# Layer 1's modulation as sums on VectorE, with moved residuals and another square

## The chip, the cores and the metric

The kernel runs on one core of one Trainium2 chip. The metric is the device time of one execution in microseconds. An execution computes two transformer blocks for 256 tokens of x (S = 256) and 256 tokens of context, model width D = 1024, all in 32-bit floats.

## The reference

Only what the change touches is kept. The first block is one layer of dilated window attention with its own modulation. The second has two layers: layer 0 mixes by retention and a gated scan, layer 1 by window attention, and each is followed by an MLP. In layer 1 the context only supplies keys and values, so its gates and its second shift and scale are not needed.

```python
def modulation(cvec, w, b):
    m = jax.nn.silu(cvec) @ w + b
    return jnp.split(m[..., None, :], 6, axis=-1)
def sublayer_residual(x, y, gate, g, b):
    return layer_norm(DEEPNORM_ALPHA * x + gate * y, g, b)
def sq_relu_mlp(h, w1, w2):
    return jnp.square(jax.nn.relu(h @ w1)) @ w2

for i in range(DEPTH_2):
    sh1, sc1, g1, sh2, sc2, g2 = modulation(c, w_mod[i], b_mod[i])
    csh1, csc1, cg1, csh2, csc2, cg2 = modulation(c_ctx, w_mod[i], b_mod[i])
    h = x * (1.0 + sc1) + sh1
    hc = xc * (1.0 + csc1) + csh1
    ...
    x = sublayer_residual(x, y, g1, ln_g[i, 0], ln_b[i, 0])
    x = sublayer_residual(x, sq_relu_mlp(x * (1.0 + sc2) + sh2, mlp_w1[i], mlp_w2[i]), g2, ln_g[i, 1], ln_b[i, 1])
    ...
```

## The kernel before, in words

**Stages.** The first block takes the first 330 us or so; the mixer of layer 0 follows; layer 0's MLP (512 tokens: context and x) runs from about 640 to 1053 us, layer 1's attention to 1195, layer 1's MLP (256 tokens) to the end at 1416.

**Order.** Each engine has one queue, worked off in order. A scheduler with a timeline simulation of its own sets the order when the kernel is built; tile pools with numbered buffers and, where given, `issue_after` edges bound what it may do. The order is fixed before the run.

**Weights and GEMMs.** Every weight of a GEMM comes in pieces of 128x1024 (`wload`): SyncE's queue loads `raw` (4 buffers), ScalarE rounds it into `whi` (L133), VectorE subtracts to get `wlo` (L134). `w_a` and `w_b` load the pieces of one weight. Each product is three matmuls (`mm3`, L157 to L159). In layer 0's MLP one `w_a` or `w_b` serves 48 matmuls of 512 columns. The accumulators are PSUM banks: three of tag `mm`, two of `S`, two of `T` (transposes), one of `O`.

**Fillers.** The modulation is a row vector times a matrix of 1024 columns for each of its parts. `quad` is a generator that streams the matrix (`mvraw`, three buffers of 128x1024, also on SyncE's queue) and multiplies it on TensorE (L239) into bank `O`, in four column tiles of 32 each; the result `R` gets its bias (`mvb`, loaded by POOL's queue), and `to_cols` (L271 and its transposes) makes columns of it. `fill(rate)` at the start of every `w_a` and `w_b` advances the generator by `rate` loads. `finish` runs a begun generator to its end, which the first block does ahead of its attention (both use bank `O`). Layer 0's modulation (`quad` with keys 0, b, c) is filled in during the first block, layer 1's during layer 0's MLP.

**The first block's attention.** For each of four head pairs (called heads below): POOL loads two tables `B` from `tabd` (two buffers), TensorE makes scores `S` (L522), VectorE reduces them with the table (L525, into `pr`, two buffers), ScalarE takes the exponential (L531), TensorE transposes `pr` (L193) and multiplies with the values into bank `O` (L545).

**The MLP.** `mlp` runs eight groups `g` of 512 hidden columns. For a group: `w_a` twice (first weight, 256 columns each), relu on ScalarE (L1001), the square as a multiplication on VectorE (L1002), `split` of the result into `fx` (a rounded half on ScalarE, the rest on VectorE, L110 and L111); then `w_b` twice (second weight), with results copied (`g` = 0, L1013) or added to `y` (L1015) by VectorE. `late` runs after group 0's square: it gives the residual stream its new values (`new_resid`: L954 times the norm's gain row, L955 plus its bias row, 128x1024 each). At the end of layer 0's MLP `after0` makes the next inputs (`modulate`: transposes, ScalarE's `hf`, VectorE's casts `hCh`, `hCh0b` at L303, rest `hCl` at L304) and two new residuals.

Of the kernel before, what the change touches and what calls it, by code (L numbers as in the profile page):

```python
# [95 lines left out]
def body(tc, a, cst, out):  # L96
    nc = tc.nc
    with ExitStack() as ctx:
# [10 lines left out]
        def split(hi, lo, src):  # L109
            nc.scalar.copy(hi, src)  # L110
            nc.vector.tensor_sub(lo, src, hi.bitcast(F32))  # L111
# [14 lines left out]
        rate = [0]  # L126

        def wload(src, k, n):
            raw = wpool.tile([P, 1024], F32, tag="raw", name="raw", bufs=4)
            nc.sync.dma_start(raw.rearrange("p (k n) -> p k n", k=k), src)  # L130
# [3 lines left out]
            nc.vector.tensor_sub(lo, raw, hi.bitcast(F32))  # L134
            return hi.rearrange("p (k n) -> p k n", k=k), lo.rearrange("p (k n) -> p k n", k=k)

        def w_a(w, col, nk=KC):

            fill(rate[0])
            ts = []  # L140
            for k0 in range(0, nk, 4):
                hi, lo = wload(w[k0 * P:(k0 + 4) * P, col:col + 256].rearrange("(k p) n -> p k n", p=P), 4, 256)
                ts += [(hi[:, k], lo[:, k]) for k in range(4)]
            return ts

        def w_b(w, col, nk=KC):

            fill(rate[0])
            ts = []
            for k0 in range(0, nk, 2):  # L150
                hi, lo = wload(w[k0 * P:(k0 + 2) * P, col:col + 512].rearrange("(k p) n -> p k n", p=P), 2, 512)
                ts += [(hi[:, k], lo[:, k]) for k in range(2)]
            return ts
# [56 lines left out]
        nc.gpsimd.memset(neghalf, -0.5)  # L210
        nc.vector.tensor_copy(cst_a[:, :, 0], cv[:, 2, :])
# [12 lines left out]
        def quad(pool, rpool, key, w, col, b, stat, vecs, n=512, rows=""):  # L224
# [32 lines left out]
            if rows:  # L257
# [3 lines left out]
                RD[rows] = rd  # L261
            yield
# [182 lines left out]
        def quad0():  # L445
            yield from quad(p1t, None, "0", w_mod[0], 0, b_mod[0], cst_m, 2)
            m0["a"] = to_cols(R["0"], "m0a")

        fillers.append(quad0())
        fillers.append(quad(p1t, const, "b", w_mod[0], 2048, b_mod[0], cst_m, 2, rows="b0"))  # L450
        fillers.append(quad(p1t, const, "c", w_mod[0], 4096, b_mod[0], cst_m, 2, rows="c0"))
# [132 lines left out]
        m0a = m0["a"]  # L584
        m0b = to_cols(R["b"], "m0b")
        m0c = to_cols(R["c"], "m0c")
# [376 lines left out]
        def mlp(layer, Ts, xks, y, pool, mid, late, norm, after):  # L963
# [4 lines left out]
            for g in range(8):  # L968
                fx = (main, pool)[g % 2].tile([P, 8, n], F32R, tag=("qkb", "fx")[g % 2], name="fx")
                fh, fl = fx[:, 0:4], fx[:, 4:8]  # L970
                if layer and g < 1:
                    ws = w_b(w1, 512 * g)
                    for i in range(2):
# [3 lines left out]
                        nc.vector.tensor_mul(f, f, o)  # L977
# [13 lines left out]
                for i in range(0 if layer and g < 1 else 2):  # L991
                    if g:
                        ws = w_a(w1, 512 * g + 256 * i)
                    for j in range(2):
# [7 lines left out]
                        nc.vector.tensor_mul(f, f, o)  # L1002
# [44 lines left out]
        m1a, m1b = {}, {}  # L1047
        fillers.append(quad(pm, pm, "0", w_mod[1], 0, b_mod[1], cst_m, 2))
        fillers.append(quad(pm, const, "b", w_mod[1], 2048, b_mod[1], cst_m, 2, rows="b1"))
        fillers.append(quad(pm, const, "c", w_mod[1], 4096, b_mod[1], cst_m, 2, rows="c1"))  # L1050
# [14 lines left out]
        rate[0] = 2  # L1065
        mod1 = {}

        def after0(T):
# [194 lines left out]
```

## Time and profile before

| what | us |
|---|---|
| median of 3 runs (1414.46 to 1416.97) | 1416.27 |
| the profiled execution | 1418.32 |
| its span (first to last instruction) | 1416.5 |
| TensorE busy | 1336.0 |
| VectorE busy | 784.4 |
| ScalarE busy | 539.1 |
| mean granted TensorE clock, as a share of full | 0.97 |

Matmuls are pipelined: the duration of one reaches into the next, so busy time of TensorE is not the same as its work. What a matmul adds to a dense row is read from start to start. The share of busy time over the whole span says little here, since the stages differ; tables of stretches come first, single instructions after.

### The profile page before, as it was taken

Reading aid. Unit: us, or ns where it says so; the run is one execution under the profiler, and the core shown is the slowest. Engines: PE = TensorE matmul, PEld = TensorE weight load, DVE = VectorE, ACT = ScalarE, POOL = GpSimd, SP = SyncE. Lnnn points to the kernel's source line nnn. Section 1 sums busy time; section 2 is a strip of 40 time slices with the busy share of each in tenths; the row PEclk is TensorE's granted clock in tenths of the full one; section 3 lists DMA queues with packets and bytes.
Section 4 is the critical chain, followed back from the end, with each engine's and each line's share of the span. In section 5 each row is a group of like instructions: output and inputs, shape, how many; then the busy total and the mean of one; then the engine's idle time right before and its main releaser. Section 6 shows DMA issues by size and latency. Waiting matters only on the chain.

```text
span 1416.5 us, 19846 instructions
## 1 busy us (share of the span) xinstructions
PE 1336.0 (94%) x7918; PEld 1054.8 (74%) x7918; DVE 784.4 (55%) x1312; ACT 539.1 (38%) x859; POOL 89.2 (6%) x138
## 2 busy tenths in 40 slices
PE   6999998999899999898999999999988899799995
PEld 5788865589787777676677767767768777698985
DVE  3534444345824348567444434344677877666666
ACT  2433434335531354214232132223235576454541
POOL 2110021000200200101000000000010000000000
PEclk9999999999989999899999999999998999899998
DMA  9888885565512411327643554553223603365651
GB/s 331 308 276 294 271 276 150 165 210 176 153 60 75 124 46 60 119 74 268 178 134 119 155 178 132 175 174 109 89 96 87 169 16 127 111 206 168 192 178 46
DMA packets 137987, 222.27 MB, mean 157 GB/s; under 512 B 8604, under 2 KB 86012, under 8 KB 137894
## 3 DMA queue, kind: packets, MB, share of 16 engines
q1 hardware_dynamic: 131984, 206.07, 46.1%
q0 software_dynamic: 5168, 14.38, 3.4%
q8 instruction: 62, 1.02, 0.3%
q10 hardware_dynamic: 742, 0.55, 0.1%
q14 instruction: 31, 0.25, 0.1%
HBM read 217.19 MB, written 1.16 MB: 154 GB/s over the span
## 4 chain that ended last, share of the span: by engine, by line
PE 87%; DVE 6%; DMA 3%; issue 2%; ACT 1%; POOL 0%; SPq 0%; DVEq 0%; ACTq 0%; POOLq 0%
PE mm L157 23%; PE mm L158 22%; PE mm L159 22%; PE O L239 5%; PE T L193 2%; DMA mvraw<-in_w_mod_dram 2%; PE mm L415 1%; PE O L1190 1%; PE S L1165 1%; DVE wlo L134 1%; PE S L522 1%; DMA raw<-in_w_in_dram 1%; PE T L747 1%; DVE st L318 1%; PE O L545 1%
## 5 line engine op out<-in xcount | busy, mean ns | idle before, releaser
L134 DVE TENSOR_TENSOR wlo<-raw,whi 128x1024 fp32r<-128x1024 f32 x261 | 318.5, 1223 | 238.1 <-ACT whi L133 236.8
L133 ACT CAST whi<-raw 128x1024 fp32r<-128x1024 f32 x261 | 273.1, 1050 | 444.1 <-PE mm L159 252.7
L157 PE MATMUL mm<-whi,fx 128*128 128x512 f32 x384 | 155.1, 404 | 3.2 <-DVE y L1015 2.2
L158 PE MATMUL mm<-wlo,fx 128*128 128x512 f32 x384 | 151.4, 394 | 0.0
L159 PE MATMUL mm<-whi,fx 128*128 128x512 f32 x384 | 144.8, 396 | 0.1
L157 PEld LDWEIGHTS mm<-whi,fx 128*128 128x128 f32 x384 | 72.2, 188 | 40.0 <-DVE y L1015 12.8
L157 PE MATMUL mm<-A1a,whi 128*128 128x256 f32 x352 | 101.0, 287 | 0.0
L159 PE MATMUL mm<-A1a,wlo 128*128 128x256 f32 x352 | 100.0, 284 | 0.0
L158 PE MATMUL mm<-A1a,whi 128*128 128x256 f32 x352 | 99.9, 284 | 0.0
L158 PE MATMUL mm<-hBl,whi 128*128 128x512 f32 (+1 forms) x256 | 97.3, 381 | 0.0
L239 PE MATMUL O<-mvraw,cst_m 128*32 128x512 f32 x384 | 80.6, 608 | 7.8 <-DMA mvraw<-in_w_mod_dram 7.8
L159 PEld LDWEIGHTS mm<-whi,fx 128*128 128x128 f32 x384 | 72.0, 188 | 19.7 <-issue 2.5
L1015 DVE TENSOR_TENSOR y<-y,mm 128x512 f32<-128x512 f32 x72 | 47.5, 684 | 67.7 <-PE mm L159 67.1
L158 PEld LDWEIGHTS mm<-wlo,fx 128*128 128x128 f32 x384 | 72.3, 188 | 15.1
L157 PEld LDWEIGHTS mm<-A1a,whi 128*128 128x128 f32 x352 | 66.3, 188 | 12.9 <-issue 11.1
L158 PEld LDWEIGHTS mm<-A1a,whi 128*128 128x128 f32 x352 | 66.3, 188 | 6.1 <-issue 6.0
L159 PEld LDWEIGHTS mm<-A1a,wlo 128*128 128x128 f32 x352 | 66.3, 188 | 3.1 <-issue 2.8
L158 PE MATMUL mm<-hDl,whi 128*128 128x256 f32 x224 | 63.0, 281 | 0.0
L1002 DVE TENSOR_TENSOR f<-f,mm 128x512 f32<-128x512 f32 (+1 forms) x58 | 32.2, 555 | 52.8 <-ACT f L1001 52.7
L1001 ACT ACTIVATE f<-mm 128x512 f32<-128x512 f32 (+1 forms) x58 | 28.5, 492 | 79.1 <-PE mm L159 78.0
L158 PEld LDWEIGHTS mm<-hBl,whi 128*128 128x128 f32 x256 | 48.1, 188 | 10.7 <-issue 0.8
L157 PE MATMUL mm<-whi,hA 128*128 128x512 f32 x128 | 51.3, 401 | 0.0
(479 smaller groups left out, 2806.9 us busy)
## 6 DMA issues: line engine op xcount, KB each, us to landing
raw<-in_mlp_w_dram SPq DMA_DIRECT2D x128, 512.0 KB, 4.2
mvraw<-in_w_mod_dram SPq DMA_DIRECT2D x96, 512.0 KB, 4.6
raw<-in_w_in_dram SPq DMA_DIRECT2D x64, 512.0 KB, 6.5
raw<-in_ev_w_in_dram SPq DMA_DIRECT2D x25, 512.0 KB, 4.6
raw<-in_od_w_qkv_dram SPq DMA_DIRECT2D x12, 512.0 KB, 3.5
mvraw<-in_w_ada_dram SPq DMA_DIRECT2D x10, 512.0 KB, 6.9
raw<-in_w_out_dram SPq DMA_DIRECT2D x8, 512.0 KB, 3.9
raw<-in_ev_w_out_dram SPq DMA_DIRECT2D x8, 512.0 KB, 3.8
```

The source lines that it names most:

```text
L133: nc.scalar.copy(hi, raw)
L134: nc.vector.tensor_sub(lo, raw, hi.bitcast(F32))
L157: nc.tensor.matmul(o, lh, rh, start=first, stop=False)
L158: nc.tensor.matmul(o, lh, rl, start=False, stop=False)
L159: nc.tensor.matmul(o, ll, rh, start=False, stop=last)
L193: nc.tensor.transpose(o, i, ident[:n, :n])
L239: nc.tensor.matmul(acc[32 * j:32 * j + 32, :n], stat[:, k, :], raw[:, j * n % 1024:j * n % 1024 + n], start=k == 0, stop=k == KC - 1)
L318: nc.vector.bn_stats(st[:, half, :], r[:, 512 * half:512 * half + 512])
L415: nc.tensor.matmul(o[:, j, :], w_[:, k, js], h_[:, 2 * p + k, :], start=(p, j, k, n) == (0, 0, 0, 0), stop=(p, k, n) == (3, 1, 2), skip_gr ...
L1001: nc.scalar.activation(f, o, AF.Relu)
L1002: nc.vector.tensor_mul(f, f, o)
L1015: nc.vector.tensor_add(y[:, T, hs], y[:, T, hs], o)
```

## The change

Five edits.

1. `fill` moves from ahead of the weights of each `w_a` and `w_b` to behind them (`fill_behind`), with an edge behind the last load of the weight (on SyncE) and behind the last `wlo` (on VectorE).
2. Layer 1's modulation is no longer made by `quad`. A new generator `summed` handles one of six parts at a time (`sh1`, `sc1` for two vectors each, `ga1`, `sh2`, `sc2`, `ga2` for one). It loads the same 48 pieces `mvraw`; VectorE multiplies each by a scalar per partition and adds it to `mva` (8 first products as tensor_scalar, 56 as scalar_tensor_tensor, 128x1024). At the end of a part the partitions are summed by matmuls with `sel` (a column of ones) into bank `O`, four to a vector, 32 in all; VectorE adds the bias, and four of the parts are transposed to columns from there. 96 matmuls of L239 and 12 transposes go. The rate is 0 in group 0's first weight, 2 after its `late`, 3 from group 3 on.
3. The square of relu is an activation on ScalarE.
4. `late` in both MLPs is queued behind `split`. The two new residuals at the end of layer 0's MLP move into layer 1's attention (behind the heads of kv = 2); at the MLP's end ScalarE copies y into their place instead. Their rows of gain and bias take buffers of the attention's pool.
5. In the first block the columns of `quad` b and c are made inside the generator, so `finish` makes those of b.

```diff
+        def fill_behind():
+            if rate[0] and queued:
+                with tc.issue_after(queued["load"]), tc.issue_after(queued["lo"]):
+                    fill(rate[0])
...
         def w_a(w, col, nk=KC):
-            fill(rate[0])
             ts = []
             for k0 in range(0, nk, 4):
                 hi, lo = wload(w[k0 * P:(k0 + 4) * P, col:col + 256].rearrange("(k p) n -> p k n", p=P), 4, 256)
                 ts += [(hi[:, k], lo[:, k]) for k in range(4)]
+            fill_behind()
             return ts
...
+        def summed(pool, res, key, w, col, b, stat, vecs, rows=False):
+            n = D // 4
+            r = pool.tile([P, n], F32, tag="mvb", name="mvb", bufs=1)
+            nc.gpsimd.memset(r, 0.0)
+            for m in range(vecs):
+                nc.gpsimd.dma_start(r[m::32, :], b[col:col + D].rearrange("(j n) -> j n", n=n))
+            accs = [pool.tile([P, D], F32, tag="mva", name="mva", bufs=2) for _ in range(vecs)]
+            wv = w.rearrange("(p k) n -> p k n", k=KC)
+            for k in range(KC):
+                raw = pool.tile([P, D], F32, tag="mvraw", name="mvraw", bufs=3)
+                nc.sync.dma_start(raw, wv[:, k, col:col + D])
+                yield
+                for m, acc in enumerate(accs):
+                    if k:
+                        nc.vector.scalar_tensor_tensor(acc, raw, stat[:, k, m:m + 1], acc, op0=ALU.mult, op1=ALU.add)
+                    else:
+                        nc.vector.tensor_scalar_mul(acc, raw, stat[:, k, m:m + 1])
+            o = bank("O")
+            for m, acc in enumerate(accs):
+                for j in range(4):
+                    nc.tensor.matmul(o[32 * j:32 * j + 32, :n], sel[:, m, :], acc[:, n * j:n * j + n], start=m == 0, stop=m == vecs - 1)
+            nc.vector.tensor_add(r, o[:, :n], r)
...
+                res[key] = to_cols(r, key, "O")
...
-        fillers.append(quad(p1t, const, "b", w_mod[0], 2048, b_mod[0], cst_m, 2, rows="b0"))
-        fillers.append(quad(p1t, const, "c", w_mod[0], 4096, b_mod[0], cst_m, 2, rows="c0"))
+        def quadcols(key, col, rows=""):
+            yield from quad(p1t, None, key, w_mod[0], col, b_mod[0], cst_m, 2, rows=rows)
+            m0[key] = to_cols(R[key], "m0" + key)
+        fillers.append(quadcols("0", 0))
+        fillers.append(quadcols("b", 2048, "b0"))
+        fillers.append(quadcols("c", 4096, "c0"))
...
+                if g == 3:
+                    rate[0] = 3
...
-                        nc.vector.tensor_mul(f, f, o)
+                        nc.scalar.activation(f, f, AF.Square)
...
                 if g == 0:
-                    late()
+                    with tc.issue_after(queued["split"]):
+                        late()
+                    rate[0] = 2
...
             modulate(y0[:, T, :], (mod1["cc"], mod1["cx"])[T // 2], mod1["h"], P * T)
-            if T == 0:
-                for t in (2, 3):
-                    new_resid(t, y0[:, t, :], mod1["ln"])
+            if T > 1:
+                nc.scalar.copy(resid(T), y0[:, T, :])
...
+            if kv == 2:
+                with tc.issue_after(queued["split"]):
+                    for T in (2, 3):
+                        new_resid(T, resid(T), lnr)
```

TensorE where layer 0's MLP begins: the last matmul of the mixer's output projection, the transposes of r, and the first matmuls of group 0. Before:

```order
L159 MATMUL mm<-whi,yL 128x512
L193 MATMUL T<-ident,r_5254 128x128 x8
L239 MATMUL O<-mvraw,cst_m 32x512 x2
L193 MATMUL T<-ident,r_5254 128x128 x4
L239 MATMUL O<-mvraw,cst_m 32x512 x2
L193 MATMUL T<-ident,r_5254 128x128 x4
L157 MATMUL mm<-hBh_5265,whi 128x256 x2
```

The same place after the change:

```order
L167 MATMUL mm<-whi,yL 128x512
L201 MATMUL T<-ident,r_5258 128x128 x16
L165 MATMUL mm<-hBh_5269,whi 128x256 x2
L165 MATMUL S<-hBh_5269,whi 128x256 x2
L166 MATMUL mm<-hBl,whi 128x256
```

The products of the modulation have gone from between the transposes.

VectorE in layer 0's MLP, while y is added up (`y_5652` and `y_5656` are the same tile). Before:

```order
L111 TENSOR_TENSOR fx<-f,fx 128x512
L1015 TENSOR_TENSOR y_5652<-y_5652,mm 128x512 x3
L255 TENSOR_TENSOR R_6415<-O,mvb 128x512
L134 TENSOR_TENSOR wlo<-raw,whi 128x1024
L1015 TENSOR_TENSOR y_5652<-y_5652,mm 128x512
L134 TENSOR_TENSOR wlo<-raw,whi 128x1024
L1015 TENSOR_TENSOR y_5652<-y_5652,mm 128x512 x3
```

After:

```order
L1062 TENSOR_TENSOR y_5656<-y_5656,mm 128x512 x3
L142 TENSOR_TENSOR wlo<-raw,whi 128x1024
L292 SCALAR_TENSOR_TENSOR mva<-mvraw,cst_m,mva 128x1024 x2
L1062 TENSOR_TENSOR y_5656<-y_5656,mm 128x512
L142 TENSOR_TENSOR wlo<-raw,whi 128x1024
L292 SCALAR_TENSOR_TENSOR mva<-mvraw,cst_m,mva 128x1024
L1062 TENSOR_TENSOR y_5656<-y_5656,mm 128x512
L292 SCALAR_TENSOR_TENSOR mva<-mvraw,cst_m,mva 128x1024
L1062 TENSOR_TENSOR y_5656<-y_5656,mm 128x512 x2
```

The multiply-adds of the sums stand among the weights' subtractions and ahead of additions to y.

TensorE in the first block where the attention's products with the values end; the stretch from the last product of `quad` b to that place is longer than can be shown. Before:

```order
L545 MATMUL O<-PT,A0a 64x128 x2
L565 MATMUL T<-qkba 128x256
L239 MATMUL O<-mvraw,cst_m 32x512 x6
L565 MATMUL T<-qkba 128x256 x2
L193 MATMUL T<-ident,Rb 128x128 x4
```

After, where `quad` b's products end:

```order
L167 MATMUL mm<-A1a,wlo 128x256
L251 MATMUL O<-mvraw,cst_m 32x512 x6
L201 MATMUL T<-ident,Rb 128x128 x4
L201 MATMUL T<-ident,pr 128x128 x6
L567 MATMUL S<-h0a 128x256 x2
```

The transposes of Rb stood behind the last head; now they stand ahead of the first transpose of `pr`.

POOL in the first block, the loads of the tables B. Before:

```order
L498 TENSOR_TENSOR qkba<-qkba 128x4x16
L509 DMA B<-tabd 128x3x256 x4
L260 DMA rdb_1858<-Rb 4x512 x2
L228 MEMSET mvb 128x512
L230 DMA mvb<-in_b_mod_dram 4x512 x2
L509 DMA B<-tabd 128x3x256 x2
```

After:

```order
L543 TENSOR_TENSOR qkba<-qkba 128x4x16
L272 DMA rdb_1862<-Rb 4x512 x2
L240 MEMSET mvb 128x512
L242 DMA mvb<-in_b_mod_dram 4x512 x2
L554 DMA B<-tabd 128x3x256 x6
```

All six reloads of B have moved behind the loads and stores of the modulation.

## Rows read from the trace of the kernel before

**Rows 1.** The page: busy us, share of the span, instructions of each engine.

```profile
PE 1336.0 (94%) x7918; PEld 1054.8 (74%) x7918; DVE 784.4 (55%) x1312; ACT 539.1 (38%) x859; POOL 89.2 (6%) x138
```

**Rows 2.** Table by stretches: start:end, length, busy of each engine (instructions), PEclk, DMA share, GB/s.

```profile
700.00:800.00 100.00, 100.00 (x436) 73.48 (x435) 42.45 (x57) 26.14 (x32) 1.67 (x3) 1.00 0.47 145
...
1047.00:1067.00 20.00, 11.55 (x57) 9.16 (x55) 19.55 (x33) 9.81 (x20) 4.09 (x6) 0.88 0.50 157
1067.00:1195.00 128.00, 122.16 (x924) 103.94 (x924) 100.08 (x249) 80.80 (x187) 3.67 (x6) 0.95 0.33 94
1195.00:1217.00 22.00, 14.43 (x48) 10.75 (x47) 19.46 (x29) 8.05 (x13) 1.67 (x3) 0.69 0.44 143
```

**Rows 3.** Groups by form, TensorE, layer 0's MLP: busy us, mean ns | idle before.

```profile
L239 PE MATMUL O<-mvraw,cst_m 128*32 128x512 f32 x188 | 39.8, 612 | 3.7 <-DMA mvraw<-in_w_mod_dram 3.7
```

**Rows 4.** Timeline, TensorE, layer 0's MLP: start, us, instruction xcount [idle before <-releaser].

```profile
644.39 1.05 PE L239 MATMUL O<-mvraw,cst_m 128*32 128x512 f32 x4 [2.56 <-DMA mvraw<-in_w_mod_dram]
...
649.22 1.81 PE L239 MATMUL O<-mvraw,cst_m 128*32 128x512 f32 x4 [3.19 <-DMA mvraw<-in_w_mod_dram]
...
786.35 0.40 PE L158 MATMUL mm<-wlo,fx 128*128 128x512 f32 x1
786.59 0.40 PE L159 MATMUL mm<-whi,fx 128*128 128x512 f32 x1
786.92 1.06 PE L239 MATMUL O<-mvraw,cst_m 128*32 128x512 f32 x8
787.91 0.66 PE L193 MATMUL T<-ident,R 128*128 128x128 f32 x4
```

**Rows 5.** Groups by form, VectorE, layer 0's MLP.

```profile
L134 DVE TENSOR_TENSOR wlo<-raw,whi 128x1024 fp32r<-128x1024 f32 x60 | 73.4, 1224 | 64.6 <-ACT whi L133 64.6
L1015 DVE TENSOR_TENSOR y<-y,mm 128x512 f32<-128x512 f32 x48 | 32.1, 685 | 55.1 <-PE mm L159 54.5
...
L1002 DVE TENSOR_TENSOR f<-f,mm 128x512 f32<-128x512 f32 x30 | 20.5, 684 | 45.2 <-ACT f L1001 45.2
...
L1019 DVE SCALAR_TENSOR_TENSOR y<-xs,y 128x1024 f32<-128x1024 f32 x2 | 2.4, 1223 | 0.0
```

**Rows 6.** Timeline, VectorE, start of layer 0's MLP.

```profile
647.47 2.36 DVE L954 TENSOR_TENSOR A1t<-r,lnr 128x1024 f32<-128x1024 f32 x2
```

**Rows 7.** Groups by form, ScalarE, layer 0's MLP.

```profile
L1001 ACT ACTIVATE f<-mm 128x512 f32<-128x512 f32 x30 | 17.8, 595 | 56.4 <-PE mm L159 56.4
```

**Rows 8.** Timelines of VectorE, then TensorE, between layer 0's MLP and the attention.

```profile
1057.91 1.22 DVE L955 TENSOR_TENSOR xs<-xs,lnr 128x1024 f32<-128x1024 f32 x1
...
1066.39 0.80 PE L157 MATMUL mm<-hCh,whi 128*128 128x256 f32 x2 [6.78 <-DVE hCh L303]
```

**Rows 9.** Timelines of VectorE, then TensorE, start of layer 1's MLP.

```profile
1204.51 1.22 DVE L954 TENSOR_TENSOR xs<-r,lnr 128x1024 f32<-128x1024 f32 x1
...
1208.31 1.21 DVE L955 TENSOR_TENSOR xs<-xs,lnr 128x1024 f32<-128x1024 f32 x1
...
1207.85 0.79 PE L157 MATMUL mm<-whi,hDh 128*128 128x512 f32 x1 [3.57 <-DVE hDh L303]
```

**Rows 10.** First block: tile Rb; POOL's timeline; chain of waits (start, us, what).

```profile
L193 PE MATMUL T<-ident,Rb x4: 273/273/328, 264.8 to 265.2; 128*128 128x128 f32 x4
...
L255 DVE TENSOR_TENSOR Rb<-O,mvb x1: 692/692/692, 222.7 to 222.7; 128x512 f32<-128x512 f32 x1
...
222.50 0.75 POOL L509 DMA_DIRECT2D B<-tabd  x1 [2.69 <-DVE m L525]
...
236.58 1.87 POOL L509 DMA_DIRECT2D B<-tabd  x2 [9.47 <-DVE m L525]
...
194.88 8.11 DMA mvraw<-in_w_mod_dram
...
236.58 5.01 DMA B<-tabd
...
261.71 1.07 PE O L239 x8
```

More of the change, by code (lines that the diff above doesn't have):

```diff
@@ L110, in split @@
             nc.scalar.copy(hi, src)
-            nc.vector.tensor_sub(lo, src, hi.bitcast(F32))
+            queued["split"] = nc.vector.tensor_sub(lo, src, hi.bitcast(F32)).ins
         fillers = []
@@ L133, in wload @@
             nc.scalar.copy(hi, raw)
-            nc.vector.tensor_sub(lo, raw, hi.bitcast(F32))
+            queued["lo"] = nc.vector.tensor_sub(lo, raw, hi.bitcast(F32)).ins
             return hi.rearrange("p (k n) -> p k n", k=k), lo.rearrange("p (k n) -> p k n", k=k)
         def w_a(w, col, nk=KC):
-            fill(rate[0])
             ts = []
@@ L152, in w_b @@
                 ts += [(hi[:, k], lo[:, k]) for k in range(2)]
+            fill_behind()
             return ts
@@ L210, in body @@
         nc.gpsimd.memset(neghalf, -0.5)
+        sel = const.tile([P, 2, 32], F32, tag="sel", name="sel")
+        nc.gpsimd.memset(sel, 0.0)
+        for m in range(2):
+            nc.gpsimd.memset(sel[:, m, m:m + 1], 1.0)
         nc.vector.tensor_copy(cst_a[:, :, 0], cv[:, 2, :])
@@ L261, in quad @@
                 RD[rows] = rd
+            yield
[10 more added lines that the diff above has]
+                nc.sync.dma_start(raw, wv[:, k, col:col + D])
+                yield
+                for m, acc in enumerate(accs):
[8 more added lines that the diff above has]
+            nc.vector.tensor_add(r, o[:, :n], r)
+            if rows:
+                rd = dram.tile([vecs, D], F32, tag="rd" + key, name="rd" + key)
+                for m in range(vecs):
+                    nc.gpsimd.dma_start(rd[m].rearrange("(j n) -> j n", n=n), r[m::32, :])
+                RD[key] = rd
+            else:
+                res[key] = to_cols(r, key, "O")
             yield
@@ L1046, in body @@
         pm = lm.enter_context(tc.tile_pool(name="pm", bufs=1, reuse_waits="tile"))
[L1047 to L1050, printed above, removed]
+        mod1 = {}
+        for i, key in enumerate(("sh1", "sc1", "ga1", "sh2", "sc2", "ga2")):
+            fillers.append(summed(pm, mod1, key, w_mod[1], D * i, b_mod[1], cst_m, 2 if i < 2 else 1, i % 3 == 2))
         lnr = ln_rows([pm.tile([P, D], F32, tag="lnr", name="lnr0", bufs=2) for _ in range(2)], (0, 0))
@@ L1190, in window @@
                     nc.tensor.matmul(op[64 * e:64 * e + 64, 0:P], vN[:, kt, 64 * kv:64 * kv + 64], PT[:, e, kt, :], start=kt == 0, stop=kt == 3)
-            nc.scalar.copy(aH[:, c, qs], op[:, 0:P])
-            nc.vector.tensor_sub(aL[:, c, qs], op[:, 0:P], aH[:, c, qs].bitcast(F32))
+            split(aH[:, c, qs], aL[:, c, qs], op[:, 0:P])
         for kv in range(4):
@@ L1199, in body @@
                     window(kv, c, qt)
+            if kv == 1:
+                lnr = ln_rows([p4.tile([P, D], F32, tag=t, name=t + "r") for t in ("kS", "lnr")], (0, 1))
+            if kv == 2:
+                with tc.issue_after(queued["split"]):
+                    for T in (2, 3):
+                        new_resid(T, resid(T), lnr)
         r1 = slot("A0", "r1", [P, 4, D])
-        m1c, m1b = mod1["c"], mod1["b"]
-        cx = mod_cols("x0b", 4, 8, m1c[:, 0:8], m1b[:, 8:16], 0)
+        cx = mod_cols("x0b", 4, 8, mod1["sc2"], mod1["sh2"], 0)
         h2 = new_h("hD")
```

32 lines of the change are left out of this document (11 added, 21 removed).

## The prediction

> **What bounds the kernel now.** I read the page first. TensorE is busy for 94% of the span, VectorE for 55% [rows 1]. That says who is short of time, not where, so the second view is the table by stretches. In the layer-0 MLP, 700 to 800 us stands for all of it: TensorE has no idle time at all, VectorE works 42.45 of 100 us [rows 2]. Whatever leaves TensorE's queue there is time saved, as long as VectorE, which gets the work, still delivers. In layer 1's window attention (1067 to 1195) TensorE is busy 122.16 and VectorE 100.08 of 128 us: little room on either. The edge between the two (1047 to 1067) is the opposite case: TensorE 11.55 of 20 us, VectorE 19.55 of 20, so there VectorE is the bound.
>
> The third view is the costliest groups in the MLP. The products of layer 1's modulation (L239) cost TensorE 39.8 us and 3.7 us of waiting for their weights [rows 3]. The mean of 612 ns times 188 would be 115 us; the instructions of one product run beside each other, so the count times the mean is not the price.
>
> **The MLP: what is removed.** One product takes TensorE from the last GEMM matmul at 786.59 to the next work at 787.91, less the pitch of 0.24 between two GEMM matmuls: 1.08 us [rows 4]. The MLP holds products worth 39.8 us by the group. At its start two of them wait for their weights, 2.56 and 3.19 us, and in after's order all sixteen transposes of r follow each other with nothing between. I expect the first GEMM matmul some 4 us earlier, which is that wait less what the inputs of the GEMM then make it wait for. Products and waits together: 39.8 + 3.7 = **-43.5**. The three groups of transposes of the modulation's rows go too; the one at 787.91 has 0.66 us, so **-2.0**.
>
> One rule of the Trainium skill bears on this price. The row shows 1.08 us for a product of four column tiles in two passes each [rows 4]. TensorE: Matmul & The Clock Gate, section "Packing small matmuls", says that matmuls in different column tiles run side by side, and that a pack spans one matmul's duration and about 4 ns for each further tile. An estimate from that and the 612 ns gives 24 products x 2 passes x 0.62 = 30 us, and the forecast would be 10 us higher. The trace agrees on the overlap, but its price is higher, and it decides.
>
> **The MLP: what is added on TensorE.** The column sums over partitions are 32 `sel` matmuls of 256 columns in eight packs of four. No row shows them; the nearest is the product of 512 columns, so a pack lies between half of 1.08 and the whole: 4.3 to 8.6, taken **+5.0**, near the half because the columns are half. Eight transposes of mvb in four pairs, each between a quarter and the half of the row's 0.66: **+1.4** (0.7 to 1.4).
>
> **The MLP: what is added on VectorE.** Fifty-six multiply-adds of 128x1024; the same form at L1019 has 1223 ns [rows 5]. Eight first products are tensor_scalar of the same size, at most that. Together about 77 us in some 360 us. The square of relu leaves VectorE: 30 x 0.684 = 20.5 us. On average VectorE goes from 42 to about 58 of 100 us, and TensorE should not notice. Within one weight call (48 matmuls x 0.233 = 11.2 us of TensorE) it is tighter: two wlo 2.45, four additions to y 2.74, and with two weights of a two-vector sum four multiply-adds 4.89 make 10.1 us, or 90%. From group 3 on, three single sums make 8.9 us, or 79%. The queue is in order, and the sums stand ahead of additions to y which free the PSUM bank of the next GEMM. A sum whose weight has not landed holds up all of that. Today the additions wait for TensorE (54.5 us for 48 of them), so there is slack of about 1.1 us each. I take **+4** for the calls where the slack doesn't do, and 0 to 20 as bounds (0.6 us for each of 32 calls at the far end).
>
> Group 0 is a case of its own. The residuals of `late0` (eight instructions of 1.22, 9.8 us) now stand after the group's split and ahead of the first copies to y; before, the first of them ran at 647.47 [rows 6], where TensorE waited for other things anyway. The `late0` work can hold TensorE for 0 to 9.8 us; the banks and the next weights cover about two thirds: **+3**.
>
> The square on ScalarE: its neighbour on that engine, the relu of the same size, has 595 ns; the multiplication on VectorE 684 [rows 5, 7]. ScalarE has 26.14 of 100 us here. I cost it at nothing; cover gone, it is at most 0.6 us a group. ScalarE: Activation LUTs, section "Rules for kernel authors", says the contrary: multiplications belong on VectorE, up to three times faster in bf16. No row here shows that for f32; it is a rival below.
>
> MLP sum: -43.5 - 2.0 + 5.0 + 1.4 + 4 + 3 = **-32**.
>
> **The edges.** Between 1049 and 1059 four residual instructions of 1.22 us stand in VectorE's queue, the last of them shown; the attention's first matmul comes after 6.78 us of idle, released by hCh [rows 8]. All four leave: at most -4.9 on VectorE, and more where the clock comes back earlier (its granted share is 0.88 in this stretch). ScalarE gets two copies of y of 128x1024 amid the casts of weights. Bounds -8 and 0, taken **-3**. At layer 1's MLP start, 1204.51 delays the cast hDh for which TensorE waits 3.57 us [rows 9]; a second one at 1208.31 stands ahead of hDh0b. Both move behind: 0 to -8 (the granted clock is 0.69 from 1195 to 1217), taken **-2.3**. The four instructions return inside the attention, where VectorE is 78% busy: **+1.5**, between 0 and 4.9.
>
> **The first block pays.** This is the step that the change's words don't tell. `finish()` now also makes the columns of quad b. In the kernel before, TensorE transposes Rb at 264.8, after the attention, though Rb is there at 222.7 [rows 10]. In after's order those four transposes stand ahead of every transpose of attention probabilities, behind all products of quad b. So the softmax of heads 0 and 1, which ran in between the products and GEMMs up to 222 us, must wait until Rb is there: the probabilities have two buffers, and only a transpose frees them. On POOL the reload of six tables B now stands behind rdb and mvb, which wait for Rb as well.
>
> When is Rb there? Its products wait for weights (8.11 us at 194.88), in three buffers; I get 217 to 221, a little earlier than before, since the heads are out of the way. How long do the heads take then? The releases of B by the reduces of two heads are at 222.50 and 236.58: a period of 14.1 to 14.5 us. Four periods from 219 end at 276; before, the attention's last work is done at 261.7. That is +15. If the heads run faster than the reload of B allows (its wait ends 5.01 us after the issue) and lose most of that, 4 x 14.3 becomes 4 x 11.5, and it is +4; if the table reloads stretch the first head also, +19. Taken **+13**. The very first products also come later, behind eight weight loads: within 2 us either way, no term.
>
> **Sum.** -32 - 3 - 2.3 + 1.5 + 13 = -22.8. The profiled execution has 1418.3 us, 2.0 above the median of 1416.27. 1418.3 - 22.8 = 1395.5; against the median **1393**. The forecast's own range, with terms a third of the way to their bounds, is 1384 to 1403.
>
> **The rivals.**
> A. VectorE becomes the bound of the MLP: the sums ahead of the additions to y, each waiting for its weight, hold the banks. Place: every weight call from group 1 on. For it: 90% in one call, an in-order queue, the weights' own queue shared with raw. Against: 42% today, and 1.1 us of slack for each addition. It wins from 27/32 = 0.84 us a call; at 1 us it costs 32 instead of 4: **1421**, slower than before.
> B. The first block is mild (+4: the reload is hidden and heads run without it) and the edges gain 8 in place of 5.3, and group 0 is covered: 1393 - 9 - 3 - 3 = **1378**. For it: quad c's products can fill holes. Against: the head period in the trace is 14.1 or more.
> C. The first block costs +19 and edges give nothing: 1393 + 6 + 5 = **1404**. For it: POOL's queue, where the reload waits longer.
> D. The change doesn't free TensorE as it says: the six `sel` packs wait for the last sum, 1.22 us and the queue before it, and the transposes for the addition. With 2.5 us at each of the six, 15 us: **1408**. Against: 23 to 27 matmuls (5 to 6 us) stand between them in the order. Here also the square that is slower on ScalarE: 16 groups x 2 x 0.684 = 22 us if exposed everywhere: 1415, chance 0.02.
>
> **Chances.** The forecast 0.48, A 0.10, B 0.22, C 0.13, D 0.07 (with the square). About 0.2%, 2.8 us, is what a measurement of this kernel can tell from no change. Faster by more than that: the forecast, B, C and 0.05 of D: 0.88. Within it: 0.02 of A near its deciding point and 0.02 of D: 0.04. Slower: the remaining 0.08 of A. Leaving out most of A and the far end of B gives the range: 1374 to 1412.
>
> **What would show it.** Right: no L239 group in the MLP's stretch, its TensorE share still 99 to 100%, the stage from the first to the last GEMM matmul about 32 us shorter; VectorE near 58 of 100 us there; the attention's first matmul less than 6 us late. In the first block the last head's end near 274 and TensorE idle before the first `T<-ident,pr`. Wrong: idle of TensorE in the MLP named for y or for sums (A); idle before O<-sel or T<-mvb (D); an attention end at 266 or earlier (B).

## The result and the profile after

The changed kernel takes 1395.61 us (median of 4 runs, 1394.03 to 1400.68) against 1416.05 for the kernel before in the same runs: a ratio of 0.9863, 95% interval 0.9836 to 0.989. The forecast was 1393, in a range of 1374 to 1412.

The two profiled executions are 1418.32 and 1394.03 us. The one is the slowest of its kernel's runs, the other the fastest, so the traces differ by 24.3 us where the medians differ by 20.4. To see where these 24.3 us arise, I take the start of the same matmul in both traces (us from the start of the span) and the change of each stretch between two such points:

| up to | before | after | gained or lost in the stretch |
|---|---|---|---|
| last product with the values, first block | 260.8 | 270.3 | +9.5 |
| last matmul of layer 0's output projection | 640.6 | 646.8 | -3.3 |
| first GEMM matmul of layer 0's MLP | 651.7 | 653.5 | -4.5 |
| its last GEMM matmul | 1058.8 | 1038.1 | -22.5 |
| first matmul of layer 1's attention | 1066.4 | 1044.7 | -1.0 |
| first transpose behind its projection | 1202.3 | 1179.6 | -1.0 |
| first matmul of layer 1's MLP | 1207.9 | 1183.4 | -1.8 |
| end of the span | 1416.5 | 1392.2 | +0.1 |

The page and the groups answer [rows 1] and [rows 3]. First the line of the page, then layer 0's MLP by form: TensorE's `sel` matmuls and transposes of mvb, VectorE's multiply-adds, ScalarE's squares (busy us, mean ns | idle before).

```profile
PE 1306.7 (94%) x7786; PEld 1058.7 (76%) x7786; DVE 823.2 (59%) x1318; ACT 575.3 (41%) x923; POOL 90.7 (7%) x144
...
L298 PE MATMUL O<-mva,sel 128*32 128x256 f32 x64 | 4.9, 390 | 0.0
L201 PE MATMUL O<-ident,mvb 128*128 128x128 f32 x8 | 1.5, 272 | 0.0
...
L292 DVE SCALAR_TENSOR_TENSOR mva<-mvraw,cst_m,mva 128x1024 f32<-128x1024 f32 x56 | 70.7, 1279 | 0.2
...
L1047 ACT ACTIVATE f<-f 128x512 f32<-128x512 f32 x32 | 20.3, 633 | 1.0
```

The products of 39.8 us have gone; in their place stand 4.9 and 1.5 us. Neither group waits for anything. VectorE works 69.7, 62.2 and 59.2 of 100 us in the three stretches from 700 to 1000 us, where 58 were forecast. The four largest of TensorE's waits in the MLP and its end, from 640 to 1050 us (who waited for whom: us in total, times, longest):

```profile
PE mm L165 <- DVE y L1060: 9.3, 1, 9.3
PE mm L165 <- DVE hCh L348: 5.3, 1, 5.3
PE T L201 <- ACT hf L346: 3.4, 2, 2.6
PE mm L165 <- DVE y L1062: 1.2, 4, 0.3
```

One wait of 9.3 us stands out, for the first copies to y. VectorE's timeline there, and the matmul that waited:

```profile
685.92 0.68 DVE L111 TENSOR_TENSOR fx<-f,fx 128x512 fp32r<-128x512 f32 x1
686.52 2.35 DVE L997 TENSOR_TENSOR A1t<-r,lnr 128x1024 f32<-128x1024 f32 x2
688.79 2.35 DVE L997 TENSOR_TENSOR xs<-r,lnr 128x1024 f32<-128x1024 f32 x2
691.06 1.28 DVE L292 SCALAR_TENSOR_TENSOR mva<-mvraw,cst_m,mva 128x1024 f32<-128x1024 f32 x1
692.26 2.35 DVE L998 TENSOR_TENSOR A1t<-A1t,lnr 128x1024 f32<-128x1024 f32 x2
694.53 2.35 DVE L998 TENSOR_TENSOR xs<-xs,lnr 128x1024 f32<-128x1024 f32 x2
696.80 1.88 DVE L1060 COPY y<-mm 128x512 f32<-128x512 f32 x3
...
697.53 0.80 PE L165 MATMUL mm<-whi,fx 128*128 128x512 f32 x1 [9.30 <-DVE y L1060]
```

VectorE is not idle for a moment: the eight residual instructions of `late0` and one multiply-add stand between the last split and the first copy. TensorE stops until the first copy has freed a bank.

In the first block, TensorE's timeline at the end of quad b, and POOL's three reloads of B behind it:

```profile
214.41 1.35 PE L251 MATMUL O<-mvraw,cst_m 128*32 128x512 f32 x4 [3.10 <-DMA mvraw<-in_w_mod_dram]
216.55 1.11 PE L201 MATMUL T<-ident,Rb 128*128 128x128 f32 x4 [0.79 <-DVE Rb L267]
217.46 1.48 PE L201 MATMUL T<-ident,pr 128*128 128x128 f32 x6
...
221.14 1.86 POOL L554 DMA_DIRECT2D B<-tabd  x2 [1.28 <-DVE m L570]
234.10 1.86 POOL L554 DMA_DIRECT2D B<-tabd  x2 [11.09 <-DVE m L570]
247.23 1.49 POOL L554 DMA_DIRECT2D B<-tabd  x2 [11.27 <-DVE m L570]
```

The transposes of pr begin only behind those of Rb, at 217.5 us, and a head takes 13.0 us (from release to release of B), where [rows 10] had 14.1.

### The profile page after: what moved, and what is told of

It reads as the page before. It is cut to its first block, busy times and chain, and to the rows that moved or that the text cites. A ratio compares the mean times of both kernels' runs of the same rounds, so it can differ in the third digit from the quotient of the medians.

```text
span 1392.2 us, 19721 instructions
## 1 busy us (share of the span) xinstructions
PE 1306.7 (94%) x7786; PEld 1058.7 (76%) x7786; DVE 823.2 (59%) x1318; ACT 575.3 (41%) x923; POOL 90.7 (7%) x144
## 4 chain that ended last, share of the span: by engine, by line
PE 84%; DVE 7%; DMA 3%; issue 2%; ACT 2%; POOL 0%; SPq 0%; DVEq 0%; ACTq 0%; POOLq 0%
PE mm L165 23%; PE mm L166 22%; PE mm L167 22%; PE O L251 3%; PE T L201 2%; PE mm L460 1%; DMA mvraw<-in_w_mod_dram 1%; DVE wlo L142 1%; PE O L1231 1%; DMA B<-tabd 1%; PE O L590 1%; PE O L429 1%; PE S L1206 1%; PE T L790 1%; DMA h1a<-in_w_ada_dram 1%
## 5 line engine op out<-in xcount | busy, mean ns | idle before, releaser
L142 DVE TENSOR_TENSOR wlo<-raw,whi 128x1024 fp32r<-128x1024 f32 x261 | 318.5, 1223 | 241.5 <-ACT whi L141 235.5
L165 PE MATMUL mm<-whi,fx 128*128 128x512 f32 x384 | 155.2, 404 | 12.7 <-DVE y L1060 9.3
L167 PE MATMUL mm<-whi,fx 128*128 128x512 f32 x384 | 148.4, 400 | 0.0
L292 DVE SCALAR_TENSOR_TENSOR mva<-mvraw,cst_m,mva 128x1024 f32<-128x1024 f32 x56 | 70.7, 1279 | 0.2
L111 DVE TENSOR_TENSOR fx<-f,fx 128x512 fp32r<-128x512 f32 (+1 forms) x60 | 34.0, 566 | 56.2 <-ACT fx L110 56.0
```

What stands on the lines that cost most here:

```text
L111: queued["split"] = nc.vector.tensor_sub(lo, src, hi.bitcast(F32)).ins
L142: queued["lo"] = nc.vector.tensor_sub(lo, raw, hi.bitcast(F32)).ins
L165: nc.tensor.matmul(o, lh, rh, start=first, stop=False)
L167: nc.tensor.matmul(o, ll, rh, start=False, stop=last)
L292: nc.vector.scalar_tensor_tensor(acc, raw, stat[:, k, m:m + 1], acc, op0=ALU.mult, op1=ALU.add)
```

## Experiments

My account after the result: the sums themselves are hidden; two things cost, the residuals of `late0` in group 0 and the place of Rb's columns in the first block. The rival account: VectorE's queue, with the sums in it, is the limit, and the wait at 688 us is one place where it shows. All runs compare with the kernel before on the same chip; 4 runs each. The runs stand on three chips, on which the kernel before took 1416.88, 1417.95 and 1417.92 us, so a difference of 1 us between two runs says nothing.

How far one trace can be trusted, the runs show themselves. VectorE's and ScalarE's queues have the same order in the first block of the changed kernel and of the two runs below that only move the late residuals; still the last product with the values starts at 270.3, 274.3 and 271.4 us. And the order is planned anew for every kernel: in layer 1's attention it comes out differently from run to run, though only the last run below edits anything there, and the way from its first matmul to its first transpose behind the projection is 134.8 to 141.1 us long. Layer 0's MLP repeats best (first to last GEMM matmul 374.2, 374.4 and 374.3 us in three kernels that have it in the same order). So a difference is read in the stage that was edited.

**Rb's columns behind the attention.** Of the changed kernel only this goes back:

```diff
-            yield from quad(p1t, None, key, w_mod[0], col, b_mod[0], cst_m, 2, rows=rows)
-            m0[key] = to_cols(R[key], "m0" + key)
+            yield from quad(p1t, p1t if key == "b" else None, key, w_mod[0], col, b_mod[0], cst_m, 2, rows=rows)
+            if key != "b":
+                m0[key] = to_cols(R[key], "m0" + key)
...
-        m0a, m0b, m0c = m0["0"], m0["b"], m0["c"]
+        m0a, m0b, m0c = m0["0"], to_cols(R["b"], "m0b"), m0["c"]
```

> The changed kernel, except that in the first block the columns of quad b are made behind the attention, as before the change (its row Rb is kept in the first block's own pool). Theory: the transposes of Rb ahead of the attention's first transpose are what moved the last product with the values from 260.8 to 270.3 us; with them behind it, that product ends at 260 to 263, the half-clock stretches from 215 to 270 shrink from 23.9 to about 10 us, and the time falls from 1395.6 by 6 to 9.5, since 6.3 of the 9.5 us were left at the start of layer 0's MLP. Rival: the loss comes from the fills that moved behind the weights, and from the products' weights landing late; then the end stays at 268 or later and the time within 2 us.

1388.58 us, ratio 0.9795 (0.977 to 0.9821): 7.0 us less than the changed kernel's median. The last product with the values starts at 257.95 us instead of 270.3. So the place of Rb's columns costs 12.4 us up to there in this pair of traces. The four later kernels with the columns at the end of the block have it at 259.0 to 263.5 us, against 270.3 to 274.3 in the three traces with the columns early: 11.5 us by the means. The kernel before, at 260.8, lies among the late ones, so no gain of the other moves shows here. POOL's reloads are back ahead of the store of Rb, which stands here between them:

```profile
219.21 0.75 POOL L555 DMA_DIRECT2D B<-tabd  x1 [24.33 <-DVE m L571]
222.65 0.75 POOL L555 DMA_DIRECT2D B<-tabd  x1 [2.69 <-DVE m L571]
223.83 1.19 POOL L272 DMA_DIRECT2D rdb<-Rb  x2 [0.43 <-DVE Rb L267]
```

The reload at 222.65 is that of the third head; in the changed kernel, 221.14 is that of the second. That is the head that was lost. The run moves TensorE's transposes and POOL's store of Rb together; which of the two holds the heads it doesn't separate. The rival of this run, the moved fills, falls.

**The late residuals without their edge.**

```diff
-                    with tc.issue_after(queued["split"]):
-                        late()
+                    if layer:
+                        with tc.issue_after(queued["split"]):
+                            late()
+                    else:
+                        late()
```

> The changed kernel without the edge that holds layer 0's late residuals behind the split; the order puts them among the casts at the start of the MLP, as before the change. Theory: the wait of 9.30 us at 688 us (released by the copy to y) is the queue of these eight instructions; it goes, with the half clock of 10.24 us behind it (5 us of work), together 14 us; the residuals then stand ahead of casts that TensorE needs at the start and give 0 to 6 back: 1382 to 1388. Rival: the copies to y wait for the sums or the weights, and the gap stays over 6 us: 1392 or more.

1391.2 us, ratio 0.9826 (0.9805 to 0.9847). The MLP from its first to its last GEMM matmul takes 376.7 us instead of 384.6. The wait of 9.3 us has gone; another has come at the start, 3.2 us for a cast's rest hBl, with three residual instructions ahead of it (VectorE, then TensorE):

```profile
658.12 2.35 DVE L997 TENSOR_TENSOR A1t<-r,lnr 128x1024 f32<-128x1024 f32 x2
660.39 1.22 DVE L997 TENSOR_TENSOR xs<-r,lnr 128x1024 f32<-128x1024 f32 x1
661.53 0.20 DVE L369 BATCH_NORM_AGGREGATE mvst<-st 128x2 f32<-128x12 f32 x1
661.65 0.64 DVE L349 TENSOR_TENSOR hBl<-hf,hBh 128x512 fp32r<-128x512 f32 x1
...
662.34 0.58 PE L166 MATMUL mm<-hBl,whi 128*128 128x256 f32 x1 [3.19 <-DVE hBl L349]
```

The time missed its range by 3 us: the trace has the MLP 7.9 us shorter, but its last product with the values starts 4 us later than that of the changed kernel, at 274.3, with the queues of VectorE and ScalarE in the same order up to there.

**The late residuals in VectorE's idle time**, behind the last input cast of the MLP:

```diff
+                queued["mod"] = nc.vector.tensor_sub(lo, hf, hi.bitcast(F32)).ins   # in modulate
...
                             mid()
+                    with tc.issue_after(queued["mod"]):
+                        late()
...
-                    with tc.issue_after(queued["split"]):
-                        late()
+                    if layer:
+                        with tc.issue_after(queued["split"]):
+                            late()
```

> The changed kernel with layer 0's late residuals queued behind the last of the MLP's input casts instead of behind the split, where VectorE had 7.0 us of idle at 667 us. Theory: nothing that TensorE waits for stands behind them; the gap of 9.30 us and its half clock go whole: 14 us, 1380 to 1384. Rival (the copies wait for sums or weights): no change, 1392 or more. If the weights' wlo behind them come too late, a new gap of 2 to 4 us at 680.

1386.34 us, ratio 0.9791 (0.9763 to 0.9818), 9.3 less than the changed kernel; the MLP takes 374.2 us, 10.3 less. The waits of TensorE from 640 to 710 us:

```profile
PE T L201 <- ACT hf L346: 3.4, 2, 2.7
PE mm L165 <- DVE y L1063: 0.5, 1, 0.5
PE mm L167 <- DVE fx L111: 0.5, 1, 0.5
```

The same sums stand in the queue, and the copies to y are on time. So it was the residuals. My 14 us were too many: I had counted half of the 10.24 us of half clock, but nearly half of that stretch lay inside the wait itself. The changed kernel's stretches (start:end, length, busy of TensorE first, then weight loads, VectorE, ScalarE, POOL; granted clock, DMA share, GB/s):

```profile
693.00:697.50 4.50, 0.00 (x0) 0.00 (x0) 4.50 (x6) 0.00 (x0) 0.00 (x0) 0.50 0.37 117
697.50:703.00 5.50, 5.46 (x13) 4.31 (x14) 2.60 (x4) 1.04 (x1) 0.00 (x0) 0.50 0.00 0
```

TensorE did nothing from 688.2 to 697.5; the granted clock fell to half (1.2 GHz) 4.7 us into that wait and stayed there for 5.5 us of work. So the clock took some 2.8 us, not 5. Wait and clock together are 12.1 us; two new waits of 0.5 us stand against them, and 0.8 us stay unexplained.

**Both moves.**

> Both of the edits of the first and the third run of this set. Theory: the two losses are in stages with a fixed distance and add: 8 + 14 = 22 us, 1372 to 1378, faster than the kernel before by 38 to 44 us. Rival: one of the two is given back at the start of the MLP: 1380 or more.

1377.87 us, ratio 0.9724 (0.971 to 0.9739): 17.7 us less than the changed kernel, against 7.0 and 9.3 apart. They add. By stages: 8.1 us less at the end of layer 0's output projection, 10.2 less in the MLP.

**Rb's columns straight behind the last head**, with both moves:

```diff
         for h2 in range(4):
             attention(h2)
+        m0["b"] = to_cols(R["b"], "m0b")
```

> Both moves of the run before (Rb's columns behind the attention, the late residuals in VectorE's idle time; 1377.9), but Rb's columns are asked for straight behind the last head instead of at the end of the block, where the order had put them at 343 us. Theory: of the 9.5 us that the changed kernel lost by the end of its attention it had 3.3 back at the end of the mixer, because the columns of b were there early: the wait for hA at 383 us was 4.67 for 5.51 us, a second one of 1.30 us was gone, and the half clock 6.8 for 10.2 us. With the columns made at 262 to 270 us both come together: 1374 to 1375. Rival: the mixer's 3.3 us come from somewhere else; then no change, 1377 to 1379.

1374.08 us, ratio 0.9699 (0.9669 to 0.9729), the fastest kernel along with the last one below. From the last product with the values to the last matmul of the output projection it is 377.7 us for 379.8. Over all traces here this stretch takes 375.7 to 377.7 us where the columns of b and of c are both made early, ahead of the heads or right behind them, and 378.7 to 380.8 where a set of them is made only at 342 to 346 us. So about 3 us go with early columns, and the changed kernel's gain in the mixer with them. What carries the 3 us isn't shown. The mixer's input hA doesn't use these columns (layer 0's MLP does), and the kernel before, which has those of b at 265 us and those of c at 346, takes 379.8 as well; the order around 345 to 390 us differs too. The rest of the 3.8 us that this run gains lies in layer 1, whose order came out differently, and isn't shown to be the columns' doing. The waits between 375 and 400 us, with both moves alone and then with the columns early:

```profile
PE mm L165 <- DVE hA L348: 5.5, 1, 5.5
PE mm L166 <- DVE hA L349: 1.3, 1, 1.3
```

```profile
PE mm L165 <- DVE hA L348: 4.7, 1, 4.7
```

**The square back on VectorE**, in the kernel with both moves, in both places where it stands in `mlp`:

```diff
-                        nc.scalar.activation(f, f, AF.Square)
+                        nc.vector.tensor_mul(f, f, o)
```

> The kernel with both moves (1377.9), with the square of relu back on VectorE as a multiplication. Theory: the squares are hidden on either engine; VectorE goes from about 64 to 69 of 100 us in layer 0's MLP, the time stays within 3 us of 1377.9. Rival (the multiplication is better off on VectorE, as the chain of relu, square and split ends sooner): up to 5 us faster. Other rival (VectorE's queue is close to its limit, so each of the squares holds up an addition): 5 to 20 us slower.

1385.64 us, ratio 0.9775 (0.9749 to 0.9802): 7.8 us slower than the kernel with both moves. My "within 3 us" fell. The layer-0 MLP takes 379.2 us for 374.4, and its only new wait is in group 0, for a split (640 to 700 us):

```profile
PE T L201 <- ACT hf L346: 3.4, 2, 2.7
PE mm L167 <- DVE fx L111: 3.4, 2, 2.9
```

The square of the second tile (672.73 us) stands behind the last residual, two subtractions of weights and the two first products of the sums, and its split (678.59) behind two subtractions more and two multiply-adds; half clock follows for 3.4 us. From group 1 on no wait of TensorE grows by more than 0.4 us. So 4.8 of the 7.8 us are explained; the rest lies in the other stages, and I can't tell it from the scatter between runs.

**No sums**: all 56 multiply-adds are left out of the kernel with both moves.

```diff
-                    if k:
-                        nc.vector.scalar_tensor_tensor(acc, raw, stat[:, k, m:m + 1], acc, op0=ALU.mult, op1=ALU.add)
-                    else:
+                    if not k:
```

> The kernel with both moves (1377.9), but only the first of the eight pieces of each part of layer 1's modulation is used: all 56 multiply-adds are left out, the loads of the weights stay. Theory: VectorE has room, so 70 us less of its work save 0 to 2 us. Rival (the queue of VectorE, with the sums ahead of additions to y, is what TensorE now waits for here and there, also without one long wait): 5 us or more, and the layer-0 MLP from its first GEMM matmul to its last falls from 374.4 to below 370 us.

1377.43 us, ratio 0.9714 (0.9682 to 0.9745): no difference from 1377.87. The MLP takes 372.4 us for 374.4: the sums cost TensorE 2.0 us there.

**The sums twice**, in the same kernel:

```diff
                         nc.vector.scalar_tensor_tensor(acc, raw, stat[:, k, m:m + 1], acc, op0=ALU.mult, op1=ALU.add)
+                        nc.vector.scalar_tensor_tensor(acc, raw, stat[:, k, 31:32], acc, op0=ALU.mult, op1=ALU.add)
```

> The kernel with both moves (1377.9), with every multiply-add of layer 1's modulation followed by a second one on a column of zeros: 56 more of 1.28 us on VectorE, 72 us, and nothing else. It prices the rival of the prediction that VectorE becomes the bound. By the account of one weight call (11.2 us of TensorE), the calls with two two-vector pieces would hold 15 us of VectorE work and those with three single pieces 12.6: if each call stands for itself, 25 to 45 us slower, about 1403 to 1423. If the slack of other calls evens it out (on average VectorE then has about 82 of 100 us), 0 to 8 us slower.

1380.99 us, ratio 0.9749 (0.9715 to 0.9783), 3.1 more than without; the intervals overlap. The MLP takes 375.5 us for 374.4, one wait for y of 1.7 us is new. First the stretch from 700 to 800 us with both moves, then with the sums twice:

```profile
700.00:800.00 100.00, 100.00 (x453) 79.00 (x453) 67.75 (x79) 34.74 (x45) 2.35 (x5) 1.00 0.55 174
```

```profile
700.00:800.00 100.00, 99.69 (x450) 78.52 (x449) 96.11 (x99) 33.36 (x42) 1.48 (x3) 1.00 0.54 165
```

VectorE works 96.11 of 100 us and TensorE stays at 99.69. The rival account is refuted: weight calls don't stand for themselves, their slack evens out.

**The fills ahead of the weights again**, in the fastest kernel:

```diff
         def w_a(w, col, nk=KC):
+            fill(rate[0])
...
-            fill_behind()
```

The same goes for `w_b`.

> The fastest kernel so far (Rb's columns behind the last head, late residuals in the idle time; 1374.1), with the fills again ahead of each weight's own loads, as before the change. Theory: the sums are hidden work and their weights have three buffers, so where they stand in the queue matters only where VectorE is needed soon: in group 0, whose order puts the sums ahead of weights and splits, a wait of 1 to 5 us; elsewhere nothing: 1374 to 1380. Rival: with a sum ahead of each weight's own subtraction, VectorE waits for the sum's weight and each of the weight calls loses about 1 us: 1395 or more.

1393.17 us, ratio 0.9835 (0.9814 to 0.9856): 19.1 us slower. The mechanism is the one I named, its size far larger. VectorE at the start of the MLP, then the matmul that waited:

```profile
638.74 2.35 DVE L142 TENSOR_TENSOR wlo<-raw,whi 128x1024 fp32r<-128x1024 f32 x2
645.55 1.42 DVE L294 TENSOR_SCALAR mva<-mvraw,cst_m 128x1024 f32<-128x1024 f32 x2 [4.45 <-DMA mvraw<-in_w_mod_dram]
646.88 0.69 DVE L363 BATCH_NORM_STATS2 st<-r 128x6 f32<-128x512 f32 x1
647.48 0.41 DVE L348 CAST hBh<-hf 128x512 fp32r<-128x512 f32 x1
...
647.95 0.80 PE L165 MATMUL mm<-hBh,whi 128*128 128x256 f32 x2 [6.15 <-DVE hBh L348]
```

VectorE stands idle for 4.45 us for a weight of the modulation, with the cast that TensorE needs behind it. Without the edges of `fill_behind` the order has put the first sums even ahead of casts of the input that the MLP's first matmul needs, though the rate is 0 in group 0's first weight. The way from the last projection matmul to the first of the MLP is 12.6 us for 6.7, the MLP 387.4 for 374.3, and every long wait of TensorE in it lies before 697 us. The four that grew, with 9.2 us more than in the fastest kernel:

```profile
PE mm L165 <- DVE y L1065: 3.2, 1, 3.2
PE mm L167 <- DVE fx L111: 2.7, 2, 1.7
PE mm L166 <- DVE hBl L349: 2.5, 1, 2.5
PE O L298 <- DVE mva L292: 1.9, 1, 1.9
```

The granted clock is at half (1.2 GHz) from 639.9 to 656.9 us and again for 3.4 us from 697.9, in the fastest kernel only from 642.0 to 648.8, which I estimate at 2 to 3 us of TensorE's work.

**The two residuals back at the edge**, in the fastest kernel:

```diff
-            if T > 1:
-                nc.scalar.copy(resid(T), y0[:, T, :])
+            if T == 0:
+                ln = ln_rows([pm.tile([P, D], F32, tag="lnr", name="lnr1", bufs=2) for _ in range(2)], (0, 1))
+                for t in (2, 3):
+                    new_resid(t, y0[:, t, :], ln)
...
-            if kv == 2:
-                with tc.issue_after(queued["split"]):
-                    for T in (2, 3):
-                        new_resid(T, resid(T), lnr)
```

> The fastest kernel so far (1374.1), with the two new residuals back at the end of layer 0's MLP instead of the copies on ScalarE and the four instructions inside the attention. Theory: the stretch from the last GEMM matmul of the MLP to the attention's first was 7.60 us in the kernel before and is 6.60 with the move; the attention with the four instructions inside is not longer (66.3 against 65.8 us up to its projection, 1.0 less in all): 1 to 2 us slower, 1375 to 1377, at the edge. Rival (the prediction's): the edge gains 3 and the attention pays 1.5: the same sum, but with the attention shorter by more than 1 us when the four leave it.

1373.42 us, ratio 0.9699 (0.9674 to 0.9724): the same. In the edited stage it is not the same: from the MLP's first GEMM matmul to the attention's first it is 381.9 us for 380.9, so the residuals cost 1.1 us at the edge, as the theory has it. The last stretch alone, 6.45 us for 6.60, hides that, for the order has pushed the wait ahead of the MLP's last matmuls (residuals at the edge, then away):

```profile
1015.29 0.66 PE L201 MATMUL T<-ident,y 128*128 128x128 f32 x4 [1.67 <-ACT hf L346]
1024.80 0.80 PE L165 MATMUL mm<-hCh,whi 128*128 128x256 f32 x2 [5.62 <-DVE hCh L348]
```

```profile
1015.35 0.50 PE L165 MATMUL mm<-whi,fx 128*128 128x512 f32 x1 [0.72 <-DVE tm L979]
1024.62 0.80 PE L165 MATMUL mm<-hCh,whi 128*128 128x256 f32 x2 [5.33 <-DVE hCh L348]
```

The time doesn't show the 1.1 us: the mixer, which the edit doesn't touch, is 2.0 us shorter in this trace. The attention is 134.8 us in both, but with its order planned anew, and the kernels with the four instructions inside have 134.8 to 141.1; so what they cost there can't be told. The rival, 3 us at the edge, falls.

## Why the prediction was right, and where its steps were not

**The sum held because its errors cancelled.** -22.8 was forecast, -20.4 is the difference of the medians, -24.3 that of the traces. By terms, in the traces: the MLP with its start -32 forecast, -27.0 found; the first block +13 forecast, +6.2 found at the mixer's end (+7.9 and +10.7 in the two runs with the same order there); the edge -3 and -1.0; the start of layer 1's MLP -2.3 and -1.8; the attention +1.5 and -1.0, of which the scatter named above leaves nothing shown. The MLP was taken 5 us too well and the first block 2 to 7 us too badly: that the sum came out is luck, the mechanisms behind its large terms are not.

**What leaves and comes on TensorE was right.** From start to start, the products in the MLP's own stretch held 39.1 us of TensorE and the twelve transposes 1.2. `sel` held 5.1, forecast 5.0; mvb 0.5, forecast 1.4, since its busy 1.5 us overlap the GEMM. 407.1 - 40.3 + 5.6 = 372.4; the kernel with both moves needs 374.4, without sums 372.4. With the start (-4.5), group 0's residuals (+10.3) and the sums (+2.0) these terms make -26.9 of the -27.0. Two more that I hadn't priced nearly cancel: the MLP's first matmuls run at half clock for 5.2 us, before for 1.1, which cost some 2 us, and the residuals' leaving gains 1.1 us at its end.

One reading of the price was wrong. The prediction says that the trace's price of a product is higher than the skill's rule. It is lower: 1.08 us in the row for a whole product, 1.24 by the prediction's estimate from the rule. The 39.1 us come from the cutting. The products stand in 32 groups of 2 to 12 instructions, and each of the 27 groups of 2, 4, 6 or 8 held TensorE for 1.06 to 1.10 us, start to start. From the chain of the kernel before (start, us, what):

```profile
681.46 0.97 PE O L239 x2
...
703.51 0.99 PE O L239 x6
...
742.97 0.98 PE O L239 x4
...
786.99 0.99 PE O L239 x8
```

That agrees with TensorE: Matmul & The Clock Gate, section "Packing small matmuls" (the Trainium skill), by which a pack spans one matmul's duration and about 4 ns for each further tile: a part of a pack is hardly cheaper than the whole. The prediction's estimate of 30 us had counted 24 whole products.

**Two terms of the MLP were mis-sized, in opposite ways.** Group 0's residuals were put at +3, "the banks and the next weights cover about two thirds". The cover was not there: 10.3 us. The sums were put at +4 (0 to 20) and cost 2.0. The bound of 20 came from setting up a balance for each weight call; the doubled sums show that the balance holds over several calls.

**The first block's mechanism was right.** The step said +13 with Rb's columns at 217 to 221 and four head periods behind them. Rb came at 215.8, the period was 13.0 for 14.3, and the place of the columns cost 12.4 us, or 11.5 by the means. What I didn't have: about 3 us come back in the mixer in every kernel with early columns, by a path that no run shows.

**One edit was not priced at all.** The fills behind the weights appear in the prediction only as the first block's late products, "no term". Undone in the fastest kernel, they cost 19.1 us. Rival A, a sum ahead of work that TensorE waits for, is real, but its place is the start of the MLP and group 0, not "every weight call from group 1 on", and this edit is what keeps it away.

**The edges were priced too high.** I took four residual instructions off a stretch where VectorE was busy 19.55 of 20 us [rows 2] and read 3 us from it. Putting them back costs 1.1 us. A busy VectorE says nothing of which instruction TensorE waits for: the first matmul of the attention still waits 5.33 us for hCh with the four away. What takes their place (ScalarE's two copies of y stand ahead of hf there) no run separates, and why the kernel before needs 7.60 us from the last GEMM matmul to the attention's first stays open.

**The square.** ScalarE: Activation LUTs, section "Rules for kernel authors" (the Trainium skill), says to multiply on VectorE. Here, in f32, the square on ScalarE takes 633 ns, the multiplication took 684 [rows 5], and moving it back makes the MLP 4.8 us longer, by a wait in group 0. The prediction had cost the move at nothing. The work ahead of the multiplication in VectorE's queue decided, not the duration of one instruction.

## What to carry to other kernels

Work taken from an engine that is busy without a break is gained to within a few per cent, if the engine that gets it has slack over several tiles; its load over a single tile is too strict a measure. What costs is the place in an in-order queue: look at the first tiles of a stage, where nothing is ahead yet, for anything (a residual, a sum waiting for its load) that stands before the first instruction that the bound engine needs. And when a generator is run to its end early, ask what its tail now stands ahead of. Where the order is planned anew for every kernel, compare stage by stage: an edit can move time in a stage that it doesn't touch.

## What the runs showed that I had not expected

- VectorE can be busy 96.11 of 100 us beside a TensorE busy for 99.69 with one more wait of only 1.7 us in the whole MLP, although TensorE needs VectorE's additions for its banks.
- The multiply-add with a scalar per partition takes 1279 ns for 128x1024, the form with a constant 1223 [rows 5]; the plain product with such a scalar 748.
- A wait of 9.3 us took 10.3 us off the stage when it went, though the clock was at half for 10.24 us: 4.7 us of these were in the wait.
